# A four-layer macaron decoder trunk on one core: the second token tile moves to eight turns behind in the attention block

## The chip, the core and the metric

The kernel runs on one core of a Trainium2 chip. Five engines work side by side, each through its own queue in strict order: TensorE (PE) for matrix products and transposes, VectorE (DVE), ScalarE (ACT), GpSimd (POOL) and SyncE (SP), which issues nearly all DMAs. The metric is the device time of one execution in microseconds; lower is better.

## The reference

One sequence of 256 tokens, width 1024, passes four layers. A layer adds half a SwiGLU of the normed input, then a mixer, then another half SwiGLU. The mixers are a gated short convolution (layers 0 and 3), latent attention (layer 1) and a spatial gating MLP (layer 2). All is float32.

```python
for i in range(DEPTH):                                      # 4
    x = x + 0.5 * swiglu(rms_norm(x, norm_g[i, 0]), ...)    # 1024 -> 2816 -> 1024
    hn = rms_norm(x, norm_g[i, 1])
    x = x + mixer_i(hn)                                     # conv, attention, gating, conv
    x = x + 0.5 * swiglu(rms_norm(x, norm_g[i, 2]), ...)

def mla_mixer(x, ...):                    # 16 heads, layer 1 only
    a = x @ w_a                           # 256 query + 128 key/value latents + 32 shared rotary
    q  = rms_norm(c_q, q_norm) @ w_uq     # 16 x 96
    kv = rms_norm(c_kv, kv_norm) @ w_ukv  # 16 x (64 key + 64 value)
    q, k = rms_norm per head, rotary on the last 32 columns
    p = softmax(q @ k.T * 96 ** -0.5, causal)
    return (p @ v) @ w_o
```

## The kernel before

**Tiles, products, units.** The tokens make two tiles of 128 (tile 0, tile 1). A float32 product is made of three passes on PE: both operands are split into a high and a low part, and high x high, high x low and low x high are added in one PSUM bank (`products`, lines 333, 334, 336). Weights come in units of 128 x 1024 values (512 KB; `w_a`'s are 832 wide, `w_uq`'s 768): a DMA on SP into one of six raw buffers (L100), the high part by ACT (L112), the low part by DVE (L123), into one of nine pairs of buffers. `Weights.order` is the list of units in the order in which a rehearsal of the program asks for them; `get` makes units ahead, up to `ahead` (4, or 3 while a tile is between two blocks), and at most two in one call. A unit is split once and read by both tiles, as long as the nine buffers hold it.

**Turns.** Each tile is a generator (`stream`); `advance` runs one turn of it. The main loop gives tile 1 and tile 0 a turn by turns, tile 1 four turns behind (`LAG`). `follow(turns)` sets another distance by pausing one tile. `later(n, f)` puts a step off by n calls of `advance`, of either tile. The order in which the code runs is the order of every queue. `own[t]` counts units that tile t is to load and split for itself; while it is positive, `unit` asks for a copy under a key of its own.

**The attention block** (`mla`, L1051). A tile's turns: four idle, four for `w_a` (L1053), two for the latents' transposes (L1058), gains (L1060, L1062) and split (L291, L292), four for keys and values (`keys`: bank emptied L1104, squares L1085, sums L1097, scale on POOL L1112 and L1114, scaled L1119 and L1121, transposed, emptied L1128), four for queries (`queries`: L1136, L1085, rotation L1046 to L1049, transposed, L1151), then waits, then scores (L1174, L1179; maximum L1182, its negative L1184, Exp L1187), two turns for each of four groups of four heads on tile 0 and one turn for each of eight groups of two heads on tile 1, then the values (transposes L299, copy L1198, products L1206, division L1212) and the product with `w_o` in `rows_into_x` (8 turns). After a block the new residual is turned for the next one, one half by DMA through DRAM (`turn_half`; gains on ACT L443) and one by PE (`turn_by_pe`, L478 on DVE), and split (L291, L292).

**The feed-forward block** ends with `rows_into_x` over 22 row blocks of `w_down`: 12 turns with units of 1024 columns, then ten with units of two row blocks and 512 columns, five for each half of the columns. In seven of the eight feed-forward blocks one chunk of gate and up goes through a side lane (`sevens`), where seven products take the place of eight on quarter blocks 11, 12, 21, 22 of the weights. The lane's steps stand between the turns of the tiles; its weights come into four block buffers in turn, first those of gate (`load_first`), then those of up (`load` inside the lane).

Of the kernel before, what the change touches and what calls it, by code (L numbers as in the profile page):

```python
# [17 lines left out]
AF = mybir.ActivationFunctionType  # L18
# [28 lines left out]
AHEAD = 4  # L47
CHAIN_AHEAD = 3
LAG = 4
CLOSE_AT, CLOSE_LAG = 10, 1  # L50
H_READ, H_TAKE = 7, 2
SEVENS, RATE = (4,), 0.6
SEVENS_TAIL = 10
# [6 lines left out]
T0_PACE = 2  # L60
C_TURN, C_WAIT = 2, 0
U_WAIT = (4, 0)
WARM = (4, 6)
MANUAL = {ET.PE, ET.Activation, ET.DVE, ET.Pool, ET.SP}
FF_CHUNKS = [(c, min(512, DFF - c)) for c in range(0, DFF, 512)]

# [101 lines left out]
def program(nc, pools, order, x, positions, norm_g, ffn_gate, ffn_up, ffn_down,  # L168
# [50 lines left out]
    credit = [0.0]  # L219
    own = [0] * NT  # L220

    def unit(t, m, k, n, c0, width):
        copy = 0
        if own[t]:
            own[t] -= 1
            copy = 1
        return W.get((m, k, n, c0, width, copy), AHEAD if not any(in_chain) else CHAIN_AHEAD)


    xs = [fixed([P, D], f"x{t}") for t in range(NT)]  # L230
# [107 lines left out]
    def linear(t, a, m, c0, width, n_kt, ps=None, k0=0, k1=None):  # L338

        ps = ps or acc()  # L340
        k = k0
        while k < (k1 or n_kt):
            w = unit(t, m, k, UNIT // width, c0, width)
            for j in range(w[2]):
                products([ps[:, :width]], a[(k + j) // 4], (k + j) % 4, w, j, [slice(0, width)], k + j == 0, k + j == n_kt - 1)
            k += w[2]
            if k < n_kt:
                yield
        return ps
# [141 lines left out]
    def normed(t, idle, evened=False):  # L491
        for _ in range(idle):
            yield
        in_chain[t] = False
        r, rms = factor(sums_of_x[t])
        last, scales[t] = scales[t], (r, rms)
        if evened:
            r = tiny(1, "evened", 8)
            nc.gpsimd.tensor_tensor(out=r, in0=scales[t][0], in1=last[1], op=ALU.mult)
        return Lhs(t), r  # L500


    def ffn(t, i, j, shared, then):
# [39 lines left out]
        def body():  # L543
            yield from linear_group(t, a, [(gate, 0, lambda ps: gate_done(0, ps)), (up, 0, lambda ps: up_done(0, ps)),
                                           (gate, 512, lambda ps: gate_done(1, ps))], 512, NK)
            for n in plain[1:]:
                c, w = FF_CHUNKS[n]
                if n > 1:
                    gate_done(n, (yield from linear(t, a, gate, c, w, NK)))
                    yield  # L550
                up_done(n, (yield from linear(t, a, up, c, w, NK)))
                yield
            if t == 0 and j == 1 and i + 1 < DEPTH:
                load_first(i + 1, 0, 6)
            yield from rows_into_x(t, lambda k: hs[k // 4], down, ks, tail, 0.5, then)
# [16 lines left out]
            events.setdefault(at - H_TAKE, []).append(lambda n=n: take(n))  # L572
        if seven and t == 0:
            events.setdefault(CLOSE_AT, []).append(lambda: follow(CLOSE_LAG))
        for at, _ in enumerate(body()):
            for event in events.get(at, ()):
                event()
            yield

    def follow(turns):  # L580

        t = int(turns > lag[0])
        pause[t] += abs(turns - lag[0])
        lag[0] = turns
# [12 lines left out]
    def load_first(i, j, every):  # L597

        raws = blocks_of[i, j] = {}
        for n, block in enumerate(("11", "12", "22", "21")):  # L600
            def load(block=block):
                raws[block] = block_of(i, j, SEVENS[0], "gate", block)

            later(1 + every * n, load)

    def sevens(i, j, chunks, shared, first):
# [5 lines left out]
        def load(u, *names):  # L612
            for name_ in names:
                if u < len(units):
                    raws[u][name_] = block_of(i, j, *units[u], name_)
# [30 lines left out]
        def sum_of(s):  # L646
            u, q = divmod(s, 7)
            if s <= last and added[q]:
                to = raws[u][right[q]]
                nc.vector.tensor_tensor(out=to, in0=to, in1=raws[u][added[q]], op=ALU.add)  # L650
# [78 lines left out]
        for s in range(last + 1):  # L729
            u, q = divmod(s, 7)  # L730

            if s + 1 <= last:
                low(s + 1)
            sum_of(s + 2)
            if q == 4:
                load(u + 1, "11", "12")
            if q == 5:
                load(u + 1, "22", "21")
            if pending:
                pending.pop(0)()  # L740
            if q == 1:
                v1 = snapshot(y)
            elif q == 3:
                v2 = snapshot(y)
            elif q == 4:
                vs = [slot([P, 512]) for _ in range(NT)]
                add(vs[0][:, :256], x, v1, ALU.add)
            elif q == 5:
                v3 = snapshot(y)
            elif q == 6:  # L750
                add(vs[1][:, 256:], z, v3, ALU.subtract)
            yield
            if q == 0:
                y = acc()
            elif q == 1:
                z = acc()
            elif q == 3:
                x = acc()
            ps = (y, z, y, x, y, y, z)[q]
            left = (a11, forms["s1"], forms.get("s2"), a12, forms.get("s3"), a22, forms.get("s4"))  # L760
            ah, al, wh, wl = left[q][0], left[q][1], forms[s][0], forms[s][1]
            for k in range(4):
                for n, (f, w) in enumerate(((ah, wh), (ah, wl), (al, wh))):
                    nc.tensor.matmul(ps[:, :256], lhsT=f[:, k, :], rhs=w[:, k, :], start=q in (0, 1, 3) and k + n == 0, stop=k == 3 and n == 2,  # L764
                                     skip_group_check=True)
            del forms[s]
            high_of(s + 2)
            if s == 0:
                low("s3")
                high_x("s4")  # L770
            if s == 1:
                low("s4")
            if q == 6:
                if u % 2 == 0:
                    pending += gate_halves(y, z, v2, vs)
                else:
                    pending += up_halves(y, z, v2, vs, chunks[u // 2], lambda: gates)
            yield
# [271 lines left out]

    def mla(t, i, ib, shared, then):  # L1051
        a, r = yield from normed(t, IDLE_MLA)
        ps = yield from linear(t, a, ("w_a", ib), 0, QL + KVL + ROPE, NK)  # L1053
        av = slot([P, QL + KVL + ROPE])
        nc.scalar.activation(av, ps[:, : QL + KVL + ROPE], AF.Copy, scale=r)
# [101 lines left out]
            keys(b, w)  # L1157
            yield
        for b in range(4):
            queries(b, unit(t, ("w_uq", ib), 0, 2, 384 * b, 384))  # L1160
            yield
        for _ in range(Q_WAIT):
            yield
# [57 lines left out]
        for h0 in range(0, HEADS, per):  # L1221
            p = scores(h0)
            later(S_TURN[t], lambda h0=h0, p=p: values(h0, p))
            for _ in range(1 if t else T0_PACE):
                yield
        for _ in range(O_WAIT[t]):
            yield
        yield from rows_into_x(t, lambda k: os_[k // 4], ("w_o", ib), range(NK), OUT_TAIL, 1.0, then)


    kinds = {"ffn": (ffn, None), "conv": (conv, None), "mla": (mla, prepare_mla), "spatial": (spatial, prepare_spatial)}
# [84 lines left out]
```

## Time and profile before

| | us |
|---|---|
| median of 3 runs | 1853.66 (1853.48 to 1860.08) |
| the profiled execution | 1853.95 |
| its span, first to last instruction | 1852.2 |
| PE busy in the span | 1826.1 |
| DVE busy | 1286.6 |
| ACT busy | 988.7 |
| POOL busy | 144.7 |

Busy times are summed over each engine's instructions. Ends of products are modelled, so a busy PE may still run below its peak; the granted clock, as a share of full speed, tells at which of its two levels it ran. A row of a timeline or of groups names the line of the kernel, the engine, the operation and the tiles, output first; after the bracket stands how long the engine was idle before it and what ended that.

### The profile page before, as it was taken

Reading aid. Unit: us, or ns where it says so; the run is one execution under the profiler, and the core shown is the slowest. Engines: PE = TensorE matmul, PEld = TensorE weight load, DVE = VectorE, ACT = ScalarE, POOL = GpSimd, SP = SyncE. Lnnn points to the kernel's source line nnn. Section 1 sums busy time; section 2 is a strip of 40 time slices with the busy share of each in tenths; the row PEclk is TensorE's granted clock in tenths of the full one; section 3 lists DMA queues with packets and bytes.
Section 4 is the critical chain, followed back from the end, with each engine's and each line's share of the span. In section 5 each row is a group of like instructions: output and inputs, shape, how many; then the busy total and the mean of one; then the engine's idle time right before and its main releaser. Section 6 shows DMA issues by size and latency. Waiting matters only on the chain.

```text
span 1852.2 us, 24827 instructions
## 1 busy us (share of the span) xinstructions
PE 1826.1 (99%) x9022; PEld 1521.3 (82%) x9022; DVE 1286.6 (69%) x1574; ACT 988.7 (53%) x1421; POOL 144.7 (8%) x279
## 2 busy tenths in 40 slices
PE   9999999999999989999999999999999999999999
PEld 7888887888888868888878888888888888878887
DVE  5555677776687666686668665778667775777773
ACT  5344545554655486554565456565456554546452
POOL 2000101000530151100010001100000000000000
PEclk9999999999999998999999999999999999999999
DMA  7678666669766841676976786656786777766674
GB/s 265 218 237 238 215 222 199 215 190 293 230 208 204 250 151 58 195 226 192 272 237 220 216 261 204 225 177 225 236 265 202 227 233 230 236 205 188 218 232 132
DMA packets 251612, 400.36 MB, mean 216 GB/s; under 512 B 25415, under 2 KB 116449, under 8 KB 251489
## 3 DMA queue, kind: packets, MB, share of 16 engines
q1 hardware_dynamic: 250480, 397.09, 68.0%
q8 instruction: 70, 1.15, 0.3%
q0 software_dynamic: 608, 1.11, 0.2%
q10 hardware_dynamic: 400, 0.57, 0.1%
q14 instruction: 54, 0.43, 0.1%
HBM read 365.67 MB, written 33.03 MB: 215 GB/s over the span
## 4 chain that ended last, share of the span: by engine, by line
PE 90%; DVE 3%; ACT 2%; DMA 2%; issue 2%; SPq 0%; ACTq 0%; DVEq 0%
PE acc L334 27%; PE acc L336 27%; PE acc L333 27%; PE acc L764 7%; PE tr L299 1%; DMA xturn<-s 1%; DVE wlo L123 1%; ACT whi L112 1%; PE acc L1206 1%; PE acc L1179 1%; DMA raw<-in_ffn_gate_dram 1%; DVE wlo L631 0%; ACT whi L626 0%; DVE s L803 0%; SPq L468 0%
## 5 line engine op out<-in xcount | busy, mean ns | idle before, releaser
L333 PE MATMUL acc<-whi,s 128*128 128x512 f32 (+2 forms) x2440 | 937.8, 384 | 2.4 <-ACT s L291 1.7
L334 PE MATMUL acc<-wlo,s 128*128 128x512 f32 (+2 forms) x2440 | 932.8, 382 | 2.7 <-DVE wlo L123 2.7
L336 PE MATMUL acc<-whi,s 128*128 128x512 f32 (+2 forms) x2440 | 896.5, 382 | 0.0
L123 DVE TENSOR_TENSOR wlo<-raw,whi 128x1024 fp32r<-128x1024 f32 (+1 forms) x580 | 685.7, 1208 | 100.9 <-ACT whi L112 98.4
L112 ACT ACTIVATE whi<-raw 128x1024 fp32r<-128x1024 f32 (+1 forms) x580 | 588.1, 1044 | 87.3 <-DMA raw<-in_ffn_down_dram 43.7
L336 PEld LDWEIGHTS acc<-whi,s 128*128 128x128 f32 x2440 | 459.1, 188 | 96.8 <-DVE s L292 1.0
L334 PEld LDWEIGHTS acc<-wlo,s 128*128 128x128 f32 x2440 | 459.4, 188 | 95.7 <-DVE wlo L123 6.9
L333 PEld LDWEIGHTS acc<-whi,s 128*128 128x128 f32 x2440 | 459.2, 188 | 92.8 <-ACT s L291 2.8
L626 ACT ACTIVATE whi<-block 128x1024 fp32r<-128x1024 f32 x98 | 103.4, 1055 | 130.6 <-DVE block L650 130.6
L764 PE MATMUL acc<-whi,s 128*128 128x256 f32 x784 | 155.4, 281 | 7.5 <-DVE s L686 7.5
L764 PEld LDWEIGHTS acc<-whi,s 128*128 128x128 f32 x784 | 127.0, 188 | 14.2 <-DVE s L686 10.5
L631 DVE TENSOR_TENSOR wlo<-block,whi 128x1024 fp32r<-128x1024 f32 x98 | 118.7, 1212 | 1.2 <-ACT whi L626 0.3
L292 DVE TENSOR_TENSOR s<-s,s 128x512 fp32r<-128x512 f32 (+1 forms) x58 | 39.9, 688 | 113.7 <-ACT s L291 112.3
L523 ACT ACTIVATE s<-acc,evened 128x512 f32<-128x512 f32 (+1 forms) x70 | 44.9, 641 | 128.0 <-PE acc L336 125.8
L411 POOL TENSOR_TENSOR total<-ss,ss 128x1 f32<-128x1 f32 x26 | 8.0, 306 | 1308.2 <-ACT s L402 1308.2
L764 PE MATMUL acc<-wlo,s 128*128 128x256 f32 x392 | 110.0, 281 | 0.0
L402 ACT ACTIVATE s<-x 128x512 bf16<-128x512 f32 x48 | 30.3, 630 | 133.3 <-DVE x L426 98.3
L325 DVE TENSOR_TENSOR s<-big,s 128x512 fp32r<-128x512 f32 x68 | 46.2, 680 | 77.6 <-ACT s L324 74.9
L532 DVE SCALAR_TENSOR_TENSOR s<-acc,evened,s 128x512 f32<-128x512 f32 (+1 forms) x70 | 48.5, 693 | 64.3 <-PE acc L336 64.3
L426 DVE SCALAR_TENSOR_TENSOR x<-acc,x 128x512 f32<-128x512 f32 x32 | 22.0, 689 | 79.8 <-PE acc L336 79.7
L764 PEld LDWEIGHTS acc<-wlo,s 128*128 128x128 f32 x392 | 73.7, 188 | 3.7
L650 DVE TENSOR_TENSOR block<-block,block 128x1024 f32<-128x1024 f32 x56 | 68.4, 1221 | 1.0
(151 smaller groups left out, 904.4 us busy)
## 6 DMA issues: line engine op xcount, KB each, us to landing
raw<-in_ffn_down_dram SPq DMA_DIRECT2D x176, 512.0 KB, 5.8
raw<-in_ffn_gate_dram SPq DMA_DIRECT2D x148, 512.0 KB, 4.5
raw<-in_ffn_up_dram SPq DMA_DIRECT2D x148, 512.0 KB, 4.6
raw<-in_conv_w_in_dram SPq DMA_DIRECT2D x48, 512.0 KB, 5.0
turn<-big SPq DMA_DIRECT2D x32, 512.0 KB, 3.1
big<-turn SPq DMA_DIRECT2D x128, 128.0 KB, 5.9
block<-in_ffn_gate_dram SPq DMA_DIRECT2D x28, 512.0 KB, 6.1
block<-in_ffn_up_dram SPq DMA_DIRECT2D x28, 512.0 KB, 6.7
```

Of the source, the lines that this page charges most:

```text
L112: self.nc.scalar.activation(hi[:, part], self.loaded[u][:, part], AF.Copy)
L123: self.nc.vector.tensor_tensor(out=lo[:, part], in0=src[:, part], in1=hi[:, part].bitcast(F32), op=ALU.subtract)
L325: nc.vector.tensor_tensor(out=lo.rearrange("p k (i b) -> p k i b", b=32), in0=src, in1=hi.bitcast(F32).rearrange("p k (i b) -> p k i b", b ...
L333: nc.tensor.matmul(ps, lhsT=ah[:, k, :], rhs=wh[:, wk, c], start=first, stop=False)
L334: nc.tensor.matmul(ps, lhsT=ah[:, k, :], rhs=wl[:, wk, c], start=False, stop=False)
L336: nc.tensor.matmul(ps, lhsT=al[:, k, :], rhs=wh[:, wk, c], start=False, stop=last)
L523: nc.scalar.activation(sg[n], ps[:, :w], AF.Silu, scale=r)
L532: nc.vector.scalar_tensor_tensor(out=h, in0=ps[:, :w], scalar=r, in1=sg[n], op0=ALU.mult, op1=ALU.mult)
L626: nc.scalar.activation(hi, src, AF.Copy)
L631: nc.vector.tensor_tensor(out=lo, in0=src, in1=hi.bitcast(F32), op=ALU.subtract)
L650: nc.vector.tensor_tensor(out=to, in0=to, in1=raws[u][added[q]], op=ALU.add)
L764: nc.tensor.matmul(ps[:, :256], lhsT=f[:, k, :], rhs=w[:, k, :], start=q in (0, 1, 3) and k + n == 0, stop=k == 3 and n == 2, skip_group_c ...
```

## The change

It has six parts. Six turns before the end of the feed-forward block ahead of attention, tile 1 is paused until it is eight turns behind, and it gets own copies of its next four units; after tile 0's attention the distance returns to four. Tile 1 also gets own copies of the first four units of `w_o`. While queries are made, fewer units are split ahead (4, 3, 2, 1), and three are split between tile 0's score groups. An Exp on one column stands at the start of tile 0's attention block. Blocks of the side lane are loaded in another order and one of them a step earlier. Three of ten warm-up products at the start go.

```diff
+MLA_LAG, MLA_OWN = 8, 4
...
-WARM = (4, 6)
+WARM = (4, 3)
...
-    def unit(t, m, k, n, c0, width):
+    def unit(t, m, k, n, c0, width, ahead=AHEAD):
...
-        return W.get((m, k, n, c0, width, copy), AHEAD if not any(in_chain) else CHAIN_AHEAD)
+        return W.get((m, k, n, c0, width, copy), min(ahead, AHEAD if not any(in_chain) else CHAIN_AHEAD))
...
+        if t == 0 and j == 0 and i % 3 == 1:
+            events.setdefault(first + full + tail - 2 - (MLA_LAG - LAG), []).append(lambda: follow(MLA_LAG, MLA_OWN))
...
-    def follow(turns):
-
+    def follow(turns, copies=0):
+
+        own[1] += copies
...
-        for n, block in enumerate(("11", "12", "22", "21")):
+        for n, block in enumerate(("21", "11", "12", "22")):
...
+            if q == 3:
+                load(u + 1, "11")
             if q == 4:
-                load(u + 1, "11", "12")
+                load(u + 1, "12", "22")
             if q == 5:
-                load(u + 1, "22", "21")
+                load(u + 1, "21")
...
     def mla(t, i, ib, shared, then):
         a, r = yield from normed(t, IDLE_MLA)
+        if t == 0:
+            nc.scalar.activation(tiny(1, "scrap", 1), half, AF.Exp)
...
-            queries(b, unit(t, ("w_uq", ib), 0, 2, 384 * b, 384))
+            queries(b, unit(t, ("w_uq", ib), 0, 2, 384 * b, 384, 4 - b))
...
             later(S_TURN[t], lambda h0=h0, p=p: values(h0, p))
+            if t == 0 and h0 >= 4:
+                W.make()
...
+        if t == 1:
+            own[t] += MLA_OWN
         yield from rows_into_x(t, lambda k: os_[k // 4], ("w_o", ib), range(NK), OUT_TAIL, 1.0, then)
+        if t == 0:
+            follow(LAG)
```

Lines of the changed kernel stand 1 further on near the top and 8 further on in `mla`'s later part.

PE's queue in the attention block, around the transposes of tile 0's latents (`s_6186`), before: `acc_6199` is tile 1's `w_a` product.

```order
L333 MATMUL acc_6199<-whi_6032,s_6113 128x416
L334 MATMUL acc_6199<-wlo_6033,s_6113 128x416
L336 MATMUL acc_6199<-whi_6032,s_6114 128x416
L299 MATMUL tr_6212<-ident,s_6186 128x128 x3
L333 MATMUL acc_6199<-whi_6063,s_6149 128x416
L334 MATMUL acc_6199<-wlo_6064,s_6149 128x416
L336 MATMUL acc_6199<-whi_6063,s_6150 128x416
```

The same place now: `acc_5581` is tile 1's last `w_down` product, `x_84` its residual, `s_6185` tile 0's latents, `acc_6258` its first keys.

```order
L335 MATMUL acc_5581<-wlo_5981,s_6013 128x512
L337 MATMUL acc_5581<-whi_5980,s_6014 128x512
L300 MATMUL tr_6209<-ident,x_84 128x128 x4
L300 MATMUL tr_6220<-ident,s_6185 128x128 x3
L334 MATMUL acc_6258<-whi_6140,s_6227 128x512
L335 MATMUL acc_6258<-wlo_6141,s_6227 128x512
L337 MATMUL acc_6258<-whi_6140,s_6228 128x512
```

Where `w_a` products of tile 1 stood around the latents' transposes, two sets of transposes now stand next to each other, and keys follow at once.

DVE's queue at the same place, before, from the residual of tile 1 (`x_84`) to the split of tile 0's latents (L292, 128x384):

```order
L426 SCALAR_TENSOR_TENSOR x_84<-acc_5584,x_84 128x512
L478 TENSOR_TENSOR s_6147<-tr_6142,columns_90 128x512
L292 TENSOR_TENSOR s_6150<-s_6147,s_6149 128x512
L123 TENSOR_TENSOR wlo_6154<-raw_5976,whi_6153 128x832
L123 TENSOR_TENSOR wlo_6166<-raw_5979,whi_6165 128x1024
L123 TENSOR_TENSOR wlo_6178<-raw_5997,whi_6177 128x1024
L1060 TENSOR_TENSOR s_6216<-tr_6212,columns_91 128x128
L1062 TENSOR_TENSOR s_6216<-tr_6212,columns_91 128x256
L292 TENSOR_TENSOR s_6220<-s_6216,s_6219 128x384
```

And now:

```order
L293 TENSOR_TENSOR s_6193<-s_6187,s_6192 128x512
L124 TENSOR_TENSOR wlo_6177<-raw_6072,whi_6176 128x768
L427 SCALAR_TENSOR_TENSOR x_84<-acc_5581,x_84 128x512
L479 TENSOR_TENSOR s_6214<-tr_6209,columns_90 128x512
L293 TENSOR_TENSOR s_6217<-s_6214,s_6216 128x512
L1068 TENSOR_TENSOR s_6224<-tr_6220,columns_91 128x128
L1070 TENSOR_TENSOR s_6224<-tr_6220,columns_91 128x256
L293 TENSOR_TENSOR s_6228<-s_6224,s_6227 128x384
```

Three weight splits moved away from between the two chains, and the residual's chain now stands directly ahead of the latents'.

ACT's queue among the queries, before (`whi_6446` and `whi_6508` are units of `w_o`):

```order
L112 ACTIVATE whi_6446<-raw_6175 128x1024
L1136 ACTIVATE s_6456<-acc_6449,rq_6240 128x384
L1085 ACTIVATE s_6459<-s_6456 128x384
L1151 ACTIVATE s_6473<-tr_6468,qk_gain 96x512
L1128 ACTIVATE s_6480<-tr_6475 96x512
L1104 ACTIVATE s_6500<-acc_6496,rkv_6338 128x512
L1085 ACTIVATE s_6503<-s_6500 128x256
L112 ACTIVATE whi_6508<-raw_6189 128x1024
```

And ACT's queue now, where the first unit of `w_o` is split (`whi_6730`):

```order
L1195 ACTIVATE s_6725,psum_6625<-acc_6715,nb_6723,fs_6257 128x128 x4
L113 ACTIVATE whi_6730<-raw_6150 128x1024
L1144 ACTIVATE s_6753<-acc_6746,rq_6511 128x384
L1093 ACTIVATE s_6756<-s_6753 128x384
L1159 ACTIVATE s_6767<-tr_6762,qk_gain 96x512
L1136 ACTIVATE s_6774<-tr_6769 96x512
L1144 ACTIVATE s_6793<-acc_6786,rq_6511 128x384
```

The splits of `w_o` moved from between tile 0's queries to behind tile 0's Exp groups, among tile 1's queries.

## Rows read from the trace of the kernel before

**Rows 1.** The page, part 2: PE's busy tenths in 40 equal slices.

```profile
PE   9999999999999989999999999999999999999999
```

**Rows 2.** Windows, us: busy time and instructions by engine, clock, DMA share, GB/s.

```profile
core 0: us, PE busy (x) PEld busy (x) DVE busy (x) ACT busy (x) POOL busy (x), PEclk, DMA share, GB/s
658.50:735.40 76.90, 68.15 (x428) 60.86 (x428) 51.84 (x132) 56.58 (x141) 30.56 (x46) 0.91 0.29 95
668.70:709.40 40.70, 32.69 (x171) 26.70 (x172) 29.37 (x88) 37.76 (x85) 29.11 (x42) 0.90 0.45 151
```

**Rows 3.** Timeline of PE in the block: start us, duration us, engine, line, operation.

```profile
658.33 0.40 PE L336 MATMUL acc<-whi,s 128*128 128x512 f32 x1
658.56 0.35 PE L333 MATMUL acc<-whi,s 128*128 128x416 f32 x1
658.75 0.35 PE L334 MATMUL acc<-wlo,s 128*128 128x416 f32 x1
...
668.68 0.50 PE L333 MATMUL acc<-whi,s 128*128 128x512 f32 x1
...
734.11 0.36 PE L1174 MATMUL acc<-causal_r,ident_r 128*128 128x256 f32 x1
...
735.12 0.48 PE L333 MATMUL acc<-whi,s 128*128 128x512 f32 x1
...
736.61 0.60 PE L299 MATMUL tr<-ident,s 128*128 128x128 f32 x4
737.05 1.00 PE L1206 MATMUL acc<-s,s 128*128 128x64 f32 x8
737.86 0.47 PE L333 MATMUL acc<-whi,s 128*128 128x512 f32 x1
```

**Rows 4.** Waits of PE, 630 to 770 us: total us, times, longest.

```profile
PE tr L299 <- DVE s L1049: 3.4, 4, 2.2
```

**Rows 5.** Timelines of ACT and DVE: both chains before the first keys.

```profile
655.97 1.28 ACT L443 ACTIVATE s<-s,columns 128x128 f32<-128x128 f32 x4
...
658.76 0.69 DVE L426 SCALAR_TENSOR_TENSOR x<-acc,x 128x512 f32<-128x512 f32 x1
660.34 0.69 DVE L478 TENSOR_TENSOR s<-tr,columns 128x512 f32<-128x512 f32 x1 [0.88 <-PE tr L299]
661.72 0.69 DVE L292 TENSOR_TENSOR s<-s,s 128x512 fp32r<-128x512 f32 x1 [0.70 <-ACT s L291]
...
667.45 0.29 DVE L1060 TENSOR_TENSOR s<-tr,columns 128x128 f32<-128x128 f32 x1 [1.63 <-PE tr L299]
...
668.11 0.52 ACT L291 ACTIVATE s<-s 128x384 fp32r<-128x384 f32 x1 [2.58 <-DVE s L1062]
```

**Rows 6.** ACT: timeline around tile 0's first Exp group; then splits, busy us, mean ns.

```profile
704.18 1.28 ACT L1187 ACT_TABLE_LOAD   x1 [0.76 <-DVE nb L1184]
705.48 0.46 ACT L1187 ACTIVATE s<-acc,nb,fs 128x128 f32<-128x128 f32 x1
...
707.23 0.68 ACT L1151 ACTIVATE s<-tr,qk_gain 96x512 f32<-96x512 f32 x1
...
L112 ACT ACTIVATE whi<-raw 128x1024 fp32r<-128x1024 f32 x9 | 9.0, 1046 | 0.0
```

**Rows 7.** DVE by line and form, 655 to 745 us: busy us, mean ns, idle.

```profile
L123 DVE TENSOR_TENSOR wlo<-raw,whi 128x1024 fp32r<-128x1024 f32 x8 | 9.7, 1219 | 1.5 <-ACT whi L112 1.5
L1182 DVE TENSOR_REDUCE mx<-acc 128x2 f32<-128x512 f32 x8 | 5.5, 687 | 5.8 <-PE acc L1179 5.8
```

**Rows 8.** Timelines of ACT and PE at the lane's change of blocks.

```profile
354.94 0.69 ACT L523 ACTIVATE s<-acc,evened 128x512 f32<-128x512 f32 x1 [0.69 <-PE acc L336]
355.52 1.05 ACT L626 ACTIVATE whi<-block 128x1024 fp32r<-128x1024 f32 x1
...
361.56 0.38 PE L764 MATMUL acc<-whi,s 128*128 128x256 f32 x1 [1.06 <-DVE s L686]
```

**Rows 9.** Timeline of PE at the start: the warm-up and the next wait.

```profile
6.09 2.67 PE L266 MATMUL acc<-ident_r 128*128 128x512 f32 x6
...
10.75 0.50 PE L333 MATMUL acc<-whi,s 128*128 128x512 f32 x1 [0.58 <-ACT whi L112]
```

## The prediction, made before the changed kernel ran

> **What bounds the kernel now.** I read the page from the top. Its second part, the span in 40 slices, has TensorE (PE) at nine tenths or more in 39 of them and lower in one, the fifteenth [rows 1]. So only three things can be won: time in which PE waits, time at its lower clock, and work that can be left out; and the change leaves out no product of the reference. The fifteenth slice is the attention block, and the list of windows shows what PE loses there. Between the first product of tile 0 with `w_a` and its first with `w_o` (658.56 to 735.12, 76.6 us [rows 3]) PE is busy 68.15 of 76.9 us, at a mean granted clock of 0.91 [rows 2]. That is 8.75 us of waits and, with 0.09 of 76.9, 6.9 us given up to the 1.2 GHz level: a ceiling of 15.7 us for anything done to this block. Within it, from the first key product on, ACT is busy 37.76 of 40.70 us while PE is busy 32.69 [rows 2]: there ACT's queue sets the pace. The list of waits names the links: transposes of queries, above all, wait for the rotation on DVE [rows 4].
>
> **What eight turns move.** The order shows the two tiles' chains further apart. I compare X, the time from tile 0's first `w_a` product to its first `w_o` product, before (76.6 us) and after. What lies inside differs. Tile 1 now enters X with its last four `w_down` units undone: 24 products of 512 columns at 0.23 us (658.33 to 658.56 [rows 3]), 5.5 us that formerly lay ahead. It leaves X with four score groups, four sets of probability transposes and four sets of value products undone that formerly were done: 4 x 1.01, 4 x 0.44 and 4 x 0.81 us (the starts 734.11, 735.12, 736.61, 737.05, 737.86 [rows 3]), 9.0 us that run beside `w_o` later. So the change of the whole time is X - 76.6 + 9.0 - 5.5 = X - 73.1. Tile 0's four turns alone ahead of the block cost nothing by this: PE takes 1.4 us for a unit there, ACT 1.05 us and DVE 1.22 us to split one [rows 6, 7].
>
> X has three parts.
> First, tile 0's `w_a` products alternate with those four `w_down` units: 24 x 0.19 (658.56 to 658.75 [rows 3]) + 5.5 = 10.1 us. In this part ACT has room, and the early Exp table goes there.
> Second, a new gap. Ahead of the first key products PE now has only two sets of transposes, and behind the last `w_down` product both tiles' chains run through the same DVE queue. Counted from the end of that product: ACT has emptied tile 0's `w_a` bank in the 1.4 us before, then has four gain multiplications (1.28 us) and a split [rows 5], so that DVE ends tile 1's first half at 1.6 us, splits a `w_uq` unit (three quarters of 1.22 [rows 7], 0.9) and comes to tile 1's residual at 2.4 us. From there the rows give residual to gains 1.58 us, of which about 0.2 is PE busy elsewhere, so 1.35; gains to low half 1.38; low half 0.6 until DVE takes tile 0's latents, which stand behind it; latents to split 0.66; split to key product 0.57 (668.11 [rows 5], 668.68 [rows 3]). Sum 7.0 us, 0.6 of it PE's transposes.
> Third, key product to `w_o`, 66.4 us before (668.68 to 735.12 [rows 3]). ACT's work up to tile 0's last Exp group is what 668.7 to 709.4 holds, 37.76 us [rows 2], less the table load (704.18 to 705.48, 1.30 us [rows 6]), less three `w_o` splits (3 x 1.05 [rows 6]) and a `w_uq` split (three quarters as wide, 0.8), plus two Exp groups (2 x 1.75, 705.48 to 707.23 [rows 6]) and two splits called among them (2.1): 38.1 us. Then come tile 1's first four score groups until `w_o`, which DVE paces: a maximum of 0.69 and a copy of the same size each, three splits of 1.22 or less [rows 7] and small ones, about 9 us. Without any further wait that is 47 us, and X = 64.
>
> **The waits that stay.** A tile's keys and queries still pass ACT, DVE and POOL in strict order, with less of the other tile's work to fill in. Following the order row by row with these durations I find ACT waiting some 8 to 9 us in the third part: behind keys at the lower clock, behind query products, and twice where DVE takes the split that the new `W.make()` calls ask for ahead of the next maximum (1.22 us [rows 7], itself behind ACT's 1.05 us after the Exp). That puts the third part at 56 us and X at 73 to 74: no gain at all. So the ends are 64 (change of -9 us) and 74 (+1). Neither row decides: ACT was busy 93% of the time in the nearest stretch [rows 2], which speaks for the low end, but with a smaller distance between the tiles, which the change gives up. I take the middle, X = 69, a change of -4 us.
>
> Two rules of the Trainium skill bear on this. The table load costs 1.30 us in [rows 6]. The page "ScalarE: Activation LUTs", section "What ACT_TABLE_LOAD costs", gives about 1.28 us and a drain of about 1.38 us for each change of set; by it moving the load is worth 2.66 us and the sum would be 1.4 us lower. For the gap: PE's granted clock is 0.90 in the second stretch of [rows 2], where its short waits lie. "TensorE: Matmul & The Clock Gate", section "HAM oscillation — how this bites in real kernels", says that idle gaps between bursts put the array back to 1.2 GHz; that speaks against a change that makes one gap of 6 us out of several short ones.
>
> **The other edits.** Eight more units are loaded and split: 8 x 1.05 us on ACT and 8 x 1.22 us on DVE [rows 6, 7]. I price them at nothing, since four fall ahead of the block and four beside `w_o`, where PE needs 1.4 us a unit; uncovered they cost up to 9.8 us. Their 4.2 MB meet DMA queues at a share of 0.29 over the block [rows 2]. The other order of blocks I price at nothing, against the look of it: in each of seven lanes PE waits 1.06 us at the change of the second block set, but the rows show ACT's block split starting right behind a SiLU that had waited for PE (354.94, 355.52), then DVE, then PE at 361.56 [rows 8]. Block loads are not late there, so earlier ones win nothing: 0 to -7.4 us, 0 taken. On SP the first block now waits for a DVE sum with a gate load queued behind it; that load stood behind a wait until later anyway. Three warm-up products fewer: the six end near 8.7 us (6.09 + 2.67), but the next wait of PE, until 10.75, is for ACT's split [rows 9], which they don't hold back: 0, bounds -1 and +2.
>
> **The sum.** The profiled execution took 1853.95 us (1852.2 of span and 1.75 around it), 0.3 us above the median of 1853.66. 1853.95 - 4 = 1850. With X from 64 to 74 this case's own range is 1845 to 1855.
>
> **Rivals.**
> Faster: the distance does what it is for. PE always has the other tile's work, no wait on DVE remains in the third part and the lower clock goes. Then X is 64 and the 1.2 GHz stretches, 0.10 of 40.7 us = 4.1 us [rows 2], go too: 1853.95 - 9 - 4 = 1841. For it: ACT could be kept 93% busy once. Against it: the 7 us gap stands in the order.
> No effect: the change doesn't do what its distance says, because both chains share DVE and POOL in any order; X = 74, 1855.
> Slower: the eight units meet a DVE that has no room. The place is tile 1's softmax beside `w_o` and the stretch where tile 0 runs alone; a softmax turn costs DVE a maximum 0.69, a copy as large, a split 1.22 [rows 7] and small ones, 2.8 us, against 1.01 + 0.44 + 0.81 [rows 3] and a `w_o` unit of 1.4, 3.7 us, on PE. From the point where DVE needs more than PE per turn, which takes a second split in each turn (4.0 us), all are uncovered: 8 x 1.22 = 9.8 us on top of X = 74, 1853.95 + 1 + 9.8 = 1865.
>
> **How the numbers follow.** Forecast 1850: 0.50. Faster rival 1841: 0.25. No effect 1855: 0.15. Slower rival 1865: 0.10. Half a per cent, about what a measurement here can tell from no change, is 9.3 us: below 1844.4 or above 1862.9. Faster by more: the faster rival and the low edge of the forecast, 0.27. Slower by more: 0.08, most of the slower rival. Within: 0.65. The range that leaves out 2 in 10 runs from the faster rival's 1841 to 1860, half way to the slower one.
>
> **What would show it.** In the profile after: X near 69; a wait of PE of about 6 us for ACT's or DVE's split just ahead of the first key products, with a granted clock well under 1 behind it; the table load ahead of `w_a`'s splits and no Exp behind one; the seven waits of 1.06 us in the lanes unchanged; no more DVE-released waits beside `w_o` than before. I am wrong if the gap isn't there, if the lanes' waits vanish, or if the time is lost or won outside the block.

## The result: 1.2% slower

| | before | after |
|---|---|---|
| median, us | 1855.09 (1853.48 to 1860.08) | 1878.06 (1874.75 to 1879.09) |
| ratio, with 95% interval | | 1.0117 [1.0104, 1.0129] |
| the profiled execution | 1853.95 | 1877.55 |
| its span | 1852.2 | 1875.8 |

The ratio is about 22 us; the two profiled executions differ by 23.6. The forecast was 1850, its range ended at 1860, and the rival on the slower side gave 1865. In what follows a ratio is turned into time with 1855 us.

### Where the 23.6 us lie

The page of the changed kernel, parts 1 and 2: busy time and instructions by engine, then PE's busy tenths and the granted clock in 40 slices. It answers to [rows 1].

```profile
PE 1831.8 (98%) x9019; PEld 1523.5 (81%) x9019; DVE 1295.9 (69%) x1582; ACT 997.4 (53%) x1430; POOL 146.0 (8%) x279
...
PE   8999999999999978999999999999999999999999
...
PEclk9999999999999988999999999999999999999999
```

PE is idle for 1875.8 - 1831.8 = 44.0 us, where it was 1852.2 - 1826.1 = 26.1: 17.9 us are new waits. The other 5.7 us are busy time, though three products fewer run: the same products at a lower clock. Nearly all of both lies in the fifteenth and sixteenth slice, the attention block. (The 8 of the first slice is 41.7 us busy of 46.9, where it was 42.4 of 46.3; that differs as much between kernels with the same warm-up.)

Windows of the changed kernel, in the columns of [rows 2]: tile 0's `w_a` products, the gap, keys to `w_o`, `w_o`, and the 35 us behind tile 0's last `w_o` product.

```profile
657.57:670.70 13.13, 11.93 (x48) 10.16 (x48) 8.05 (x9) 8.37 (x14) 0.00 (x0) 0.87 0.55 180
670.70:678.19 7.49, 1.18 (x9) 0.75 (x8) 4.09 (x8) 3.23 (x9) 0.00 (x0) 0.86 0.49 178
678.19:741.50 63.31, 51.65 (x307) 46.53 (x308) 38.23 (x107) 44.84 (x114) 28.75 (x46) 0.88 0.26 84
741.50:760.83 19.33, 19.33 (x139) 17.53 (x137) 12.44 (x20) 9.37 (x22) 0.00 (x0) 1.00 0.24 82
760.83:796.00 35.17, 31.18 (x138) 24.87 (x137) 26.73 (x36) 20.95 (x35) 6.24 (x10) 0.90 0.58 187
```

Timeline of PE in the changed kernel, in the columns of [rows 3], with the idle time before a product and what ended it: the entry of the block, the gap, the first product with `w_o`, and the place behind tile 0's last.

```profile
653.69 0.50 PE L335 MATMUL acc<-wlo,s 128*128 128x512 f32 x1 [0.77 <-DVE wlo L124]
...
657.57 0.46 PE L334 MATMUL acc<-whi,s 128*128 128x416 f32 x1 [1.05 <-ACT s L292]
659.23 0.72 PE L335 MATMUL acc<-wlo,s 128*128 128x416 f32 x1 [1.20 <-DVE wlo L124]
...
670.50 0.40 PE L337 MATMUL acc<-whi,s 128*128 128x512 f32 x1
674.28 0.66 PE L300 MATMUL tr<-ident,x 128*128 128x128 f32 x4 [3.38 <-DVE x L427]
...
678.19 0.80 PE L334 MATMUL acc<-whi,s 128*128 128x512 f32 x1 [2.93 <-ACT s L292]
...
741.50 0.48 PE L334 MATMUL acc<-whi,s 128*128 128x512 f32 x1
...
762.52 0.98 PE L300 MATMUL tr<-ident,s 128*128 128x128 f32 x4 [1.30 <-ACT s L1195]
...
766.39 1.11 PE L300 MATMUL tr<-ident,s 128*128 128x128 f32 x4 [2.05 <-DVE s L450]
```

X, the prediction's stretch from `w_a` to `w_o`, is 741.50 - 657.57 = 83.9 us where it took 69. By the prediction's own formula the change is X - 73.1 = +10.8 us, where it took -4. The rest of the 23.6 us lies outside X:

- 2.2 us come before the block: the same product starts at 630.17 before and at 632.33 after. This isn't the change's doing, as the early-Exp experiment shows below.
- 2.4 us come at the entry. With the 5.5 us that moved into X and the 2.2 us above, tile 0's first `w_a` product should start at 658.56 - 5.5 + 2.2 = 655.2, and it starts at 657.57. The waits of 0.77 and 1.05 us stand there.
- 8.2 us, what is left, come behind the first `w_o` product. The fifth window holds nearly all: 4.0 us of idle PE, and 0.10 of 35.2 us, 3.5 us, of lower clock.

Set against the kernel before, X itself lost more ahead of the first key product than behind it. Of tile 1's `w_a` products 24 lie behind that product now, where it was 6, so 18 x 0.19 = 3.4 us moved there. At the old pace the stretch ahead of it would be 10.1 + 5.5 - 3.4 = 12.2 us and the stretch behind it 66.4 - 9.0 + 3.4 = 60.8. They are 20.6 us (8.4 more) and 63.3 us (2.5 more).

The list of waits of PE between 600 and 800 us of the changed kernel, its first eight lines, answering to [rows 4]: total us, times, longest.

```profile
PE tr L300 <- DVE s L1055: 5.4, 4, 2.2
PE acc L334 <- ACT s L292: 4.0, 2, 2.9
PE tr L300 <- DVE x L427: 3.4, 1, 3.4
PE acc L335 <- DVE wlo L124: 2.5, 3, 1.2
PE tr L300 <- ACT s L1195: 2.3, 2, 1.3
PE tr L300 <- DVE s L1129: 2.3, 1, 2.3
PE tr L300 <- DVE s L450: 2.0, 1, 2.0
PE tr L300 <- DVE s L1220: 2.0, 1, 2.0
```

The wait for the rotation (L1055, L1049 before) is not gone but 2.0 us longer than its 3.4 [rows 4]. Each of the seven other kinds is new or larger than before; no single one is the loss.

### The profile page after: what moved, and what is told of

Same layout as the page of the kernel before. It is cut to its first block, busy times and chain, and to the rows that moved or that the text cites. A ratio compares the mean times of both kernels' runs of the same rounds, so it can differ in the third digit from the quotient of the medians.

```text
span 1875.8 us, 24864 instructions
## 1 busy us (share of the span) xinstructions
PE 1831.8 (98%) x9019; PEld 1523.5 (81%) x9019; DVE 1295.9 (69%) x1582; ACT 997.4 (53%) x1430; POOL 146.0 (8%) x279
## 4 chain that ended last, share of the span: by engine, by line
PE 80%; DVE 8%; ACT 4%; DMA 4%; issue 3%; SPq 0%; POOL 0%; DVEq 0%; ACTq 0%
PE acc L335 24%; PE acc L337 24%; PE acc L334 24%; PE acc L770 6%; DVE wlo L124 3%; DMA raw<-in_ffn_gate_dram 2%; ACT whi L113 1%; DVE wlo L635 1%; PE tr L300 1%; DMA xturn<-s 1%; ACT whi L630 1%; ACT s L1195 1%; DVE block L654 1%; DVE s L533 1%; ACT s L292 0%
## 5 line engine op out<-in xcount | busy, mean ns | idle before, releaser
L334 PE MATMUL acc<-whi,s 128*128 128x512 f32 (+3 forms) x2440 | 939.8, 385 | 6.1 <-ACT s L292 4.4
L335 PE MATMUL acc<-wlo,s 128*128 128x512 f32 (+3 forms) x2440 | 934.6, 383 | 5.4 <-DVE wlo L124 5.3
L337 PE MATMUL acc<-whi,s 128*128 128x512 f32 (+3 forms) x2440 | 897.7, 382 | 0.0
L124 DVE TENSOR_TENSOR wlo<-raw,whi 128x1024 fp32r<-128x1024 f32 (+2 forms) x588 | 695.1, 1208 | 113.4 <-ACT whi L113 111.9
L113 ACT ACTIVATE whi<-raw 128x1024 fp32r<-128x1024 f32 (+2 forms) x588 | 595.9, 1044 | 95.0 <-DMA raw<-in_ffn_down_dram 53.0
```

Source lines behind the costliest of these rows:

```text
L113: self.nc.scalar.activation(hi[:, part], self.loaded[u][:, part], AF.Copy)
L124: self.nc.vector.tensor_tensor(out=lo[:, part], in0=src[:, part], in1=hi[:, part].bitcast(F32), op=ALU.subtract)
L334: nc.tensor.matmul(ps, lhsT=ah[:, k, :], rhs=wh[:, wk, c], start=first, stop=False)
L335: nc.tensor.matmul(ps, lhsT=ah[:, k, :], rhs=wl[:, wk, c], start=False, stop=False)
L337: nc.tensor.matmul(ps, lhsT=al[:, k, :], rhs=wh[:, wk, c], start=False, stop=last)
```

## The experiments

Theory A: the distance of eight turns makes the loss. Theory B: the later output units make it. Each part of the change was first put into the kernel before by itself, or taken out of the changed kernel. Diffs are cut, with `...` at the cuts; line numbers differ by a few from kernel to kernel.

**The distance alone**

```diff
+MLA_LAG, MLA_OWN = 8, 4
+            events.setdefault(first + full + tail - 2 - (MLA_LAG - LAG), []).append(lambda: follow(MLA_LAG, MLA_OWN))
+            own[t] += MLA_OWN
+            follow(LAG)
```

> Only the distance of eight turns with its eight copied units is put into the kernel before; Exp table, output units, blocks and warm-up stay as before. Theory A (the distance makes the loss: tile 0's keys, queries and score groups find too little of tile 1 beside them): 1868 to 1880, and the stretch from the first key product to the first w_o product near 63 us. Theory B (the output units split among tile 0's score groups make it): under 1862, that stretch under 58 us.

Measured: 1874.64, ratio 1.0109 [1.0092, 1.0126], some 20 us. The stretch from the first key product to the first `w_o` product is 61.4 us.

**The change without the distance**

```diff
-MLA_LAG, MLA_OWN = 8, 4
+MLA_LAG, MLA_OWN = 4, 0
```

> The changed kernel with the distance left at four turns and no copies; all else of the change stays. Theory A: 1850 to 1858, so within 0.2% of the kernel before. Theory B: 1865 or more, because the late output units are still there.

Measured: 1859.12, 1.0021 [1.0005, 1.0037], some 4 us. The distance makes most of the loss, but not all.

**The later output units alone**

```diff
+            queries(b, unit(t, ("w_uq", ib), 0, 2, 384 * b, 384, 4 - b))
+            if t == 0 and h0 >= 4:
+                W.make()
```

> Only the later output units (fewer units ahead among the queries, three made among tile 0's score groups) are put into the kernel before. Theory A: within 3 us of the kernel before. Theory B: 1860 to 1875, with ACT or DVE splits ahead of the maxima of tile 0.

Measured: 1861.10, 1.0028 [1.0015, 1.0042], some 5 us. Theory A expected less than 3; theory B is right that these lines cost something.

**The change without the later output units**

```diff
-            queries(b, unit(t, ("w_uq", ib), 0, 2, 384 * b, 384, 4 - b))
+            queries(b, unit(t, ("w_uq", ib), 0, 2, 384 * b, 384))
-            if t == 0 and h0 >= 4:
-                W.make()
```

> The changed kernel with the output units split as early as before; the distance of eight turns stays. Theory A: within 4 us of the changed kernel, 1872 to 1880. Theory B: 1855 to 1865.

Measured: 1874.42, 1.0105 [1.0086, 1.0123]. Within the change these lines are worth some 2 us, an amount that the two intervals don't separate from nothing.

**The early Exp alone**

```diff
+        if t == 0:
+            nc.scalar.activation(tiny(1, "scrap", 1), half, AF.Exp)
```

> Only the early Exp on one column is put into the kernel before, so that ACT's table load leaves the place between tile 0's first maximum and its first Exp. The profiles with and without it differ by about 2 us within the attention block. If ACT's chain sets the pace there as the prediction says: 1.3 to 2.7 us below the kernel before, about 1852. If the load was hidden: no difference.

Measured: 1854.52, 0.9996 [0.9988, 1.0005]: -0.7 us, no difference that is shown. Its profile shows something else. Row of the timeline of PE of this kernel, whose code is that of before up to the attention block:

```profile
661.03 0.35 PE L334 MATMUL acc<-whi,s 128*128 128x416 f32 x1
```

Tile 0's first `w_a` product starts here 2.5 us later than the 658.56 of before [rows 3]; in the two other kernels with the same code up to there (the later output units alone, and the one unit behind each score group below) it starts at 660.8 and 660.2. So the 2.2 us ahead of the block differ from one execution to the next and are not of the change: the profiled execution of before was an early one.

**Block order and warm-up alone**

```diff
-        for n, block in enumerate(("11", "12", "22", "21")):
+        for n, block in enumerate(("21", "11", "12", "22")):
...
+            if q == 3:
+                load(u + 1, "11")
...
-WARM = (4, 6)
+WARM = (4, 3)
```

> Only the order of the side lane's blocks, the earlier load and the three warm-up products fewer are put into the kernel before. The prediction priced both at nothing: within 2 us of the kernel before, the seven waits of 1.06 us in the lanes unchanged. If the block order makes the half-microseconds to 1.7 us that the profile of the changed kernel lost near 485 us: 1 to 4 us above.

Measured: 1857.17, 1.0008 [0.9999, 1.0018]: nothing that is shown.

So the distance had to be taken apart.

**Six and five turns**, both against the distance alone

```diff
-MLA_LAG, MLA_OWN = 8, 4
+MLA_LAG, MLA_OWN = 6, 2
```

> The distance alone, but six turns and two copied units at each of the two places instead of eight and four. Theory A1 (each turn of distance takes work away from beside tile 0's chain): about half the loss, 1862 to 1867. Theory A2 (the loss comes with the pause and the return themselves, whatever their size): 1870 or more.

```diff
-MLA_LAG, MLA_OWN = 8, 4
+MLA_LAG, MLA_OWN = 5, 1
```

> Five turns and one copied unit at each place. If the loss grows evenly from four turns on, as six and eight turns suggest: 1858 to 1862. If five still finds room: within 2 us of the kernel before.

Measured: 1864.27 with six, 1.0049 [1.0035, 1.0063]; 1862.28 with five, 1.0032 [1.0019, 1.0046]. Some 6, 9 and 20 us for five, six and eight turns: the loss grows with the distance. Not all of it is one mechanism. With five turns it is the rotation of the queries that PE waits for, as its list of waits (600 to 810 us) shows; before, it was 3.4 us [rows 4]:

```profile
PE tr L300 <- DVE s L1053: 10.9, 7, 4.2
```

**Eight turns whose copies cost nothing**, against the distance alone

```diff
     def get(self, key, ahead):
+        if key[-1]:
+            return self.stand_in(key)
```

> The distance of eight turns alone, with tile 1's eight copied units neither loaded nor split: its products read a pair of buffers of the same shape that another unit left there, so its output isn't the reference's. Theory A (the distance itself): 1868 to 1875. Theory C (the eight more loads and splits on SP, ACT and DVE make the loss): under 1862, with no late w_down load ahead of the block and the residual of tile 0 no longer behind a split after its w_o.

Measured: 1867.41, 1.0063 [1.0049, 1.0077]. Neither theory in full: the eight loads and splits cost 20.2 - 11.7 = 8.5 us, the distance 11.7. (Each ratio is known to about 3 us either way, a difference of two to about 4.) In its profile PE has no wait at the entry, and tile 0's first `w_a` product starts at 654.88, where it starts at 657.42 with the distance alone. Behind tile 0's last `w_o` product the waits stay, and a unit's low part still stands ahead of tile 0's residual there. Timeline of PE of this kernel:

```profile
755.43 0.98 PE L310 MATMUL tr<-ident,s 128*128 128x128 f32 x4 [1.32 <-ACT s L1201]
...
759.30 1.11 PE L310 MATMUL tr<-ident,s 128*128 128x128 f32 x4 [1.71 <-DVE s L460]
```

**Only the copies of `w_o` cost nothing**, against the kernel just shown

```diff
-        if key[-1]:
+        if key[-1] and key[0][0] == "w_o":
             return self.stand_in(key)
```

> The distance of eight turns alone; of the eight copied units only the four of w_o are neither loaded nor split (tile 1's products read another unit's buffers, so the output isn't the reference's). All eight left out were worth some 7 us. If the four late w_down units carry most of it: 1871 to 1875. If the four of w_o, among the softmax, do: 1867 to 1870.

Measured: 1873.91, 1.0092 [1.0076, 1.0109]. By this the four of `w_o` are worth some 3 us, which the intervals don't separate from nothing, and the four of `w_down` some 5. In the profiles tile 0's first key product starts at 678.58 with the distance alone, at 679.14 here and at 672.95 with none of the copies: 5.6 us and more for `w_down`.

**The return ahead of the scores**, against the distance alone

```diff
             load_first(i, 1, 4)
+            follow(LAG)
         for h0 in range(0, HEADS, per):
...
-        if t == 1:
-            own[t] += MLA_OWN
...
-        if t == 0:
-            follow(LAG)
```

> The distance of eight turns alone, but it returns to four ahead of tile 0's first score group instead of after its product with w_o; so the four copies of w_o fall away. Theory R (part of the loss is the return itself: tile 0 stands still while tile 1's last score groups have nothing beside them, some 7 us by the profiles): 1862 to 1869, and no wait of PE behind tile 0's last w_o product. Theory P (a return costs the same wherever it stands): 1871 or more.

Measured: 1865.22, 1.0050 [1.0035, 1.0065], 11 us less than with the late return. Windows from the first key product to the first `w_o` product, and from there to the first product of 512 columns behind the next side lane, in the columns of [rows 2]: first with the late return (the distance alone), then with the early one.

```profile
678.58:740.01 61.43, 51.21 (x308) 45.04 (x308) 38.26 (x107) 46.52 (x115) 27.85 (x46) 0.87 0.27 87
740.01:905.98 165.97, 161.14 (x879) 137.23 (x878) 120.95 (x143) 90.88 (x134) 5.99 (x10) 0.98 0.58 185
```

```profile
678.99:746.03 67.04, 58.72 (x396) 53.17 (x396) 44.92 (x122) 51.24 (x132) 28.17 (x46) 0.91 0.26 80
746.03:895.50 149.47, 148.22 (x791) 125.94 (x790) 110.23 (x125) 81.97 (x113) 5.06 (x10) 1.00 0.62 191
```

With the late return 9.0 us of tile 1's work stand in the second window instead of the first, as the prediction had it. So of the 10.9 us between the two kernels 61.4 + 9.0 - 67.0 = 3.4 lie in the first window, where the early return gives tile 0's score groups more of tile 1 beside them, and 166.0 - 9.0 - 149.5 = 7.5 in the second. With the early return the second window is as long as before (149.54 us from 735.12). Of the early kernel's list of waits of PE (600 to 810 us) only this one lies behind its first `w_o` product:

```profile
PE tr L300 <- DVE s L450: 0.2, 1, 0.2
```

**One unit behind each score group, none taken from the queries**

```diff
+            if t == 0 and h0 >= 4:
+                W.make()
```

> The kernel before, with four units ahead among the queries as before, and one unit made behind each of tile 0's last three score groups. Theory S1 (a split behind an Exp group and ahead of the next maximum costs the 7 us of the later output units): 1859 to 1864. Theory S2 (it is that splits are taken out of the queries, and so crowd the softmax): within 2 us of the kernel before.

Measured: 1866.56, 1.0057 [1.0042, 1.0071], some 11 us, more than either theory gave and more than with fewer units ahead as well (5). So it is a split behind an Exp group that costs, not the splits taken out of the queries; why it costs more without those is open. ACT's, then DVE's, then PE's timeline of this kernel:

```profile
727.74 1.07 ACT L113 ACTIVATE whi<-raw 128x1024 fp32r<-128x1024 f32 x1
728.69 0.61 ACT L292 ACTIVATE s<-tr 128x512 fp32r<-128x512 f32 x1
...
729.33 0.69 DVE L293 TENSOR_TENSOR s<-tr,s 128x512 fp32r<-128x512 f32 x1 [2.52 <-ACT s L292]
729.94 1.22 DVE L124 TENSOR_TENSOR wlo<-raw,whi 128x1024 fp32r<-128x1024 f32 x1
731.07 0.68 DVE L1186 TENSOR_REDUCE mx<-acc 128x2 f32<-128x512 f32 x1
...
732.05 0.56 ACT L1191 ACTIVATE s<-acc,nb,fs 128x256 f32<-128x256 f32 x1 [2.75 <-DVE nb L1188]
...
732.75 0.98 PE L300 MATMUL tr<-ident,s 128*128 128x128 f32 x4 [2.55 <-ACT s L1191]
```

ACT takes the unit first and the split of the attention output (L292) behind it. DVE waits 2.52 us for that, then splits the unit's low part, and only then comes the maximum on which Exp and PE's transposes wait.

**Less distance than four**

```diff
-MLA_LAG, MLA_OWN = 8, 4
+MLA_LAG, MLA_OWN = 3, 0
```

> The distance goes to three turns instead of eight in the attention block, no copies. Six turns cost about half of what eight cost. Theory A1 (less distance is better throughout): 1849 to 1853. Theory O (four is about the best: nearer, both tiles' chains stand in the same stretch of DVE's and ACT's queues): 1857 or more.

Measured: 1855.62, 0.9993 [0.9983, 1.0002], no difference that is shown. Then three and two turns, each with the early Exp; these diffs too are against the distance alone, and the Exp stands in both:

```diff
-MLA_LAG, MLA_OWN = 8, 4
+MLA_LAG, MLA_OWN = 3, 0
...
+            nc.scalar.activation(tiny(1, "scrap", 1), half, AF.Exp)
```

> Distance three in the attention block and the early Exp, nothing else of the change. Three turns alone were 0.07% and the early Exp alone 0.04% below the kernel before, neither beyond its interval. If both are real and add up: 1.5 to 2.5 us below the kernel before. If they are noise: no difference.

```diff
-MLA_LAG, MLA_OWN = 8, 4
+MLA_LAG, MLA_OWN = 2, 0
```

> The same with distance two. If the loss per turn of distance goes on below four: 2 to 4 us below the kernel before. If the two tiles' chains meet on DVE: above the kernel before.

Measured: 1853.74, 0.9986 [0.9977, 0.9994] with three, and 1855.81, 0.9995 [0.9986, 1.0004] with two. Three turns with the early Exp is the one version that comes out below both kernels, by some 2.6 us; the last section tells why that is no proof for the distance.

## Why the prediction was wrong, step by step

The changed kernel's profiled execution took 27.6 us more than the forecast of 1850. X took 14.9 us more than the 69: 3.0 in its first part, 0.5 in the gap, 11.4 in the third part. The other 12.8 us lie outside X, where the sum had no term or put it at nothing; 2.2 of them differ between executions.

**What bounded the kernel, and where the change acts: right.** Nothing else moved beyond what differs between executions. The seven lane waits are as they were (7.5 us in 7), as the part on block order said, and block order and warm-up measured within the bounds.

**The gap: right.** Forecast 7.0 us with 0.6 of PE; the second window has 7.5 with 1.2. The waits of 3.38 and 2.93 us stand where the order put them. The prediction cited the Trainium skill, "TensorE: Matmul & The Clock Gate", section "HAM oscillation — how this bites in real kernels", against the change. The trace agrees: the products behind the gap start 0.43 us apart (678.78, 679.21) and are back at 0.23 by 682.97; the window of the gap has a clock of 0.86.

**The first part: too small by 3 us.** 13.1 us instead of 10.1: a wait of 1.20 us for a `w_a` unit's low part and a clock of 0.87. This belongs to the copies, next.

**"I price them at nothing": failed, 8.5 us.** The cover was put in DVE's and ACT's time per turn (1.22 and 1.05 us against 1.4 on PE), which is right as a rate. The 8.5 us are those of the distance alone. What failed first was the load. ACT's timeline in the changed kernel:

```profile
642.23 4.84 ACT L113 ACTIVATE whi<-raw 128x1024 fp32r<-128x1024 f32 x5
...
651.32 1.06 ACT L113 ACTIVATE whi<-raw 128x1024 fp32r<-128x1024 f32 x1 [3.73 <-DMA raw<-in_ffn_down_dram]
```

With the copies each tile takes a unit of its own per turn, and five splits in a row, begun only when tile 0's residual was through, used up what had been loaded. SP issued the next `w_down` load only at 646.28, right behind the DMAs that turn tile 0's half through DRAM (from 642.34 on), a place where the kernel before had a `w_a` unit that was not needed so soon; ACT waited 3.73 us for it, the `w_a` units stood behind it, and the entry lost 2.4 us. Without the copies that wait and the late start were gone. The four of `w_o` cost some 1 to 3, as the rival on the slower side said in kind, but its reason shows little: behind tile 0's `w_o` PE has one wait for a low part, 0.53 us at 777.15, and with the distance alone its like (0.62 us) goes when these copies cost nothing.

**The third part: failed, 63.3 us instead of 51 to 52.** It was built on ACT's work with 8 to 9 us of ACT's own waits as the upper end, and then the middle was taken. The work was right, the waits were not. Window from the first key product to the end of tile 0's last Exp group:

```profile
678.19:731.05 52.86, 42.35 (x240) 37.65 (x241) 31.34 (x94) 39.50 (x100) 28.75 (x46) 0.89 0.26 87
```

ACT's work in it is 39.5 us, forecast 38.1; its idle time is 52.86 - 39.50 = 13.4 us, and over the whole third part 63.31 - 44.84 = 18.5. ACT's timeline at the first Exp of tile 0's four groups:

```profile
707.44 0.46 ACT L1195 ACTIVATE s<-acc,nb,fs 128x128 f32<-128x128 f32 x1 [2.53 <-DVE nb L1192]
...
714.05 0.46 ACT L1195 ACTIVATE s<-acc,nb,fs 128x128 f32<-128x128 f32 x1 [1.16 <-DVE nb L1192]
...
722.95 0.46 ACT L1195 ACTIVATE s<-acc,nb,fs 128x128 f32<-128x128 f32 x1 [2.08 <-DVE nb L1192]
...
729.29 0.46 ACT L1195 ACTIVATE s<-acc,nb,fs 128x128 f32<-128x128 f32 x1 [2.97 <-DVE nb L1192]
```

These are 8.7 us; before, ACT waited 0.76 us at the first group [rows 6] and 1.65 at all four. ACT "busy 93%" [rows 2] was true only as long as the other tile's work stood in its queue; with the tiles further apart the chain maximum, negative, Exp, transposes sets the pace, and each link waits for the one before it. That bringing tile 1 nearer ahead of the score groups takes 3.4 us off this stretch (the experiment on the return) speaks for the same. What failed here is a gain that did not come, more than a loss: against 60.8 us at the old pace this part is 2.5 us longer, and with the distance alone, at 61.4, 0.6. PE's part of the same stretch: 11.7 us idle, and 0.12 of 63.3 us, 7.6 us, given up to the lower level; the sum had named that level only behind the gap. The effect of `W.make()` was named in the right place and at the right size of one wait (ACT's 1.05 and DVE's 1.22 us); what the sum left out is the lower clock that can follow such a wait, which the last section shows in another kernel.

**The return to four turns: missing, 7 to 8 us.** The prediction asked what is late next inside X and stopped at `w_o`. After `w_o` tile 0 stands still for four turns, and tile 1's last Exp group, its transposes and the values of its last two groups have too little beside them. ACT's and DVE's timelines of the changed kernel, behind tile 0's last `w_o` product (760.83):

```profile
761.81 0.56 ACT L1195 ACTIVATE s<-acc,nb,fs 128x256 f32<-128x256 f32 x1 [2.75 <-DVE nb L1192]
...
763.99 1.22 DVE L124 TENSOR_TENSOR wlo<-raw,whi 128x1024 fp32r<-128x1024 f32 x1 [1.67 <-ACT whi L113]
765.13 0.68 DVE L425 TENSOR_TENSOR x<-acc,x 128x512 f32<-128x512 f32 x1
765.85 0.49 DVE L450 TENSOR_SCALAR s<-x,rstd 128x512 f32<-128x512 f32 x1
```

Tile 0's residual (L425) could have run from about 761.2 on. It runs at 765.13, because a unit's low part stands ahead of it, waiting for ACT, which waits for tile 1's maximum. PE waits 1.30 and 2.05 us and then runs at the lower level until about 771.8. This fills the place that the slower rival named, tile 1's softmax beside `w_o`, by another mechanism: not DVE's room for eight more units, since the waits stay without the copies, but a tile that is held; with the early return they are gone.

**The early Exp: right in place, small in worth.** The table load moved to 660.54, with two of `w_a`'s eight splits ahead of it and the others behind:

```profile
660.54 1.28 ACT L1060 ACT_TABLE_LOAD   x1
```

Alone it gave -0.7 us, with -2.2 and +0.9 as the interval's ends. The 2.66 us that the Trainium skill's "ScalarE: Activation LUTs", section "What ACT_TABLE_LOAD costs", would give lie beyond that. Both ACT timelines show the 1.28 us of the load; that ACT's time was not all on the path here is the likely reason, which no run isolates.

**The sum by experiments.** The distance's 20.2 us lie at the two ends. The copies of `w_down` are 5 to 6 us, ahead of the first key product. What stands behind the first `w_o` product is 7 to 8, of which the copies of `w_o` are 1 to 1.5 by the profiles (the second window is 166.0 us with all copies, 164.5 without these, 165.0 without any). The third part is 0.6. Some 6 to 7 are left. The likely place is the gap, 6.3 us of waits in the changed kernel, where PE was idle 0.7 us between tile 0's first `w_a` and first key product before; no run takes it out by itself. The later output units add 2, the early Exp takes off about 1, block order and warm-up add 1 or 2; that is within the measurement of the change's 22. Why five turns already cost 6 us isn't settled beyond the wait for the rotation shown above.

## What to carry to other kernels

Moving two interleaved streams apart must be costed at three places, at the pause, between, and at the return; here the return held one tile just where the other's softmax had little beside it, and moving it ahead of the scores made the kernel with the distance alone 11 us faster. An engine that is busy 93% in a profile isn't the bound of a schedule in which the work that kept it busy is moved away: follow the chain of one stream alone, link by link, and count every instruction that stands ahead of a link in a strict queue with the time for which that instruction itself waits. Units that are taken twice can use up what has been loaded in a few turns, even where the engines' rates allow them: look at what stands ahead of the next load in its queue.

## What the runs showed of the hardware

The lower clock is not a fixed price of a wait. Windows from tile 0's first key product to its first `w_o` product, first in the kernel with three turns and the early Exp, then in that with the early Exp alone:

```profile
671.10:733.60 62.50, 52.86 (x381) 46.31 (x379) 45.54 (x123) 50.37 (x133) 29.19 (x42) 1.00 0.31 102
```

```profile
671.10:736.95 65.85, 58.73 (x381) 52.36 (x379) 45.54 (x124) 50.36 (x133) 29.34 (x42) 0.90 0.30 97
```

The same 381 products. The first has more idle PE time (9.6 us against 7.1) and yet ran at 2.4 GHz throughout; the second, like the kernel before (0.90 [rows 2]), fell to the lower level for a part. It gave up 0.10 of 65.85 us, 6.6 us, to that level, more than the whole difference of 3.35 us between the two. The clock differs between executions of one kernel too. Of the twelve of three turns with the early Exp, four had a mean clock of 1.000 over the span and took 1849.3 to 1853.2 us; eight had 0.996 to 0.999 and took 1853.4 to 1857.4. Of the ten with the later output units alone, one had 0.999 and took 1853.85; the four at 0.994 took 1861.5 to 1864.6. In the profile of the kernel with the later output units alone PE waits 2.55 us for an Exp, until 728.98, and behind it stands this window:

```profile
731.00:743.00 12.00, 12.00 (x58) 12.00 (x58) 4.57 (x10) 2.40 (x8) 0.00 (x0) 0.50 0.01 1
```

That is twelve microseconds at 1.2 GHz with PE busy throughout, 6 us of work given up behind a wait of 2.55. So part of the cost of the later output units is clock, and the 2.6 us of three turns with the early Exp may be a clock that stayed up more often. Which waits bring the clock down in an execution stays open.
